# Pinning the second half of an encoder block to its source order and writing it as one pipeline of block pairs

## The chip, the cores and the metric

The kernel runs on one core of one Trainium2 chip. The metric is the device time of one execution in microseconds (us). Before the change it is 1429.65 us, the median of 3 runs (1428.54 to 1430.14).

## The reference

One layer of an encoder works on x, 256 tokens by 2048 channels, all in float32. Cut to what matters:

```
h    = rms_norm(x, g_mix)
proj = h @ w_in                        # q, k, v of three token mixers, and three gates of 2048
oa, ob, oc = mixer A (dilated windows), mixer B (grouped heads, rotary), mixer C (256 memory tokens)
gates  = sigmoid(gt)                   # (256, 3, 2048)
merged = gates[0]*(oa @ w_br_a) + gates[1]*(ob @ w_br_b) + gates[2]*(oc @ w_br_c)
x  = x + merged @ w_o
hf = rms_norm(x, g_ffn) @ w_ffn_in     # 2 x 5632 columns
x  = x + (silu(hf[:, :5632]) * hf[:, 5632:]) @ w_ffn_out
```

## The kernel before, in words

Every matrix product is cut into column blocks of 512 and runs over k tiles of 128 rows. To keep float32 accuracy each operand is split in two halves that TensorE takes at full rate: `split` (lines 83 to 91) lets ScalarE copy the source into the upper half (`hi`) and then lets VectorE subtract it from the source to get the lower half (`lo`). One product of a k tile is three matmuls: upper by upper, upper by lower, lower by upper. Weights come raw from memory on SyncE's queue (SP) and are split on the way; `whi` and `wlo` have four buffers of two k tiles each.

`product` (lines 161 to 188) computes one column block for the 256 tokens, which are two row tiles (t = 0, 1), in two banks of PSUM. It loads 1 MB (four k tiles) at a time into one of three `raw` buffers. Line 157 is the load, lines 86 and 87 the split, lines 183 to 185 the matmuls. After every k tile it calls `tick`, which lets a background job (attention, say) trace its next few instructions.

The stages in order: the memory tokens' keys and values (`w_mem`); eight blocks of q, k, v with attention in the background (`w_qkv`); twelve blocks of gates, each followed by a short branch product (`w_gate`, `w_br`), a sigmoid and a merge into `mg`; four blocks of the output projection (`w_o`), each followed by an add to x, squares for the norm, and transposes into x1T; eleven feed-forward blocks in three groups (4, 4, 3), each group followed by four blocks of `w_ffn_out`. The loop over gates has three passes, one for each branch: A (k tiles 0 and 1 of the attention output oT), C (2 to 5), B (6 to 11). The second pass begins at 380.9 us, the output projection at 612.2, the feed-forward part at 711.2.

A feed-forward block (`in_seven`, lines 525 to 615) makes 512 columns of both halves of hf at once, from 16 k tiles in eight units of two. For three of the units (`SEVEN`) the 2 by 2 arrangement of two row tiles and two column blocks is computed with seven products in place of eight. Those need stationary sums of x1T (`stationary_forms`, lines 507 to 523) and, on VectorE, sums of weights: t3, a sum into `raw`, t2 and t4. The other five units are plain ("d"). The strings `ORDER` and `ORDER0` give the order of the units; "6", "7" and "4" are the products that take t2, t3 and t4. At the end six adds and subtractions (lines 609 to 614) bring the partial sums X, Y, Z, W, V, Q together, then come SiLU (line 623), the product of the two halves (line 624), transposes (line 229) and a split into hT. PSUM is given out anew before this part: seven banks for sums, one for transposes.

The order in which each engine issues its instructions isn't that of the source: a planner that simulates the time (`schedule_with_timeline_sim=True`) takes, on each engine, what it expects to be ready. Once planned, the order on an engine is fixed, and an instruction that waits holds up all behind it.

Of the kernel before, what the change touches and what calls it, by code (L numbers as in the profile page):

```python
# [18 lines left out]
P = 128  # L19
# [8 lines left out]
PK, LOAD = 2, 4  # L28
# [24 lines left out]
ORDER = "s0 d3 s1 d4 s2 d5 6 d6 7 d7 4".split()  # L53
ORDER0 = "d3 d4 d5 s0 s1 d6 s2 6 d7 7 4".split()
# [3 lines left out]
def encoder_block(ctx: ExitStack, tc: tile.TileContext, a: dict, out: bass.AP):  # L58
    nc = tc.nc
# [6 lines left out]
    banks = ExitStack()  # L66
    pools = {"mm": banks.enter_context(tc.tile_pool(name="pmm", bufs=4, space=bass.MemoryType.PSUM)),
             "at": banks.enter_context(tc.tile_pool(name="pat", bufs=4, space=bass.MemoryType.PSUM))}
# [7 lines left out]
    def at_bank(name):  # L76
        return pools["at"].tile([P, NC], F32, name=name, tag="at")

    def mm_bank(name="mm"):
        return pools["mm"].tile([P, NC], F32, name=name, tag="mm")  # L80
# [69 lines left out]
    def load(src, k0, nk):  # L150

        raw = wp.tile([P, LOAD, NC], F32, name="raw")
        if nk % PK:
            c = k0 % PK * NC
            nc.sync.dma_start(out=raw[:, 0], in_=src[k0 // PK][:, c:c + NC])
        else:
            nc.sync.dma_start(out=raw[:, :nk].rearrange("p (u k) n -> p u (k n)", k=PK),
                              in_=src[k0 // PK:(k0 + nk) // PK].rearrange("u p n -> p u n"))
        return raw

    def product(src, lhs, nk, head=(), beside={}):


        ps = [mm_bank() for _ in range(T)]
        k0 = 0
        while k0 < nk:
            n = head[0] if head else min(LOAD, nk - k0)
            head = head[1:]
            if k0 in beside:
                start(beside[k0])  # L170
            lhs(k0)
            raw = load(src, k0, n)
            for b in range(0, n, PK):
                m = min(PK, n - b)
                hi = wp.tile([P, PK, NC], F32R, name="whi", bufs=4)
                lo = wp.tile([P, PK, NC], F32R, name="wlo", bufs=4)
                split(hi[:, :m], lo[:, :m], raw[:, b:b + m])
                for i in range(m):
                    k = k0 + b + i
                    xh, xl = lhs(k)  # L180
                    for t in range(T):
                        c = slice(t * P, (t + 1) * P)
                        nc.tensor.matmul(ps[t], lhsT=xh[:, c], rhs=hi[:, i], start=(k == 0), stop=False)  # L183
                        nc.tensor.matmul(ps[t], lhsT=xh[:, c], rhs=lo[:, i], start=False, stop=False)  # L184
                        nc.tensor.matmul(ps[t], lhsT=xl[:, c], rhs=hi[:, i], start=False, stop=(k == nk - 1))  # L185
                    tick()
            k0 += n
        return ps
# [34 lines left out]
    def transposed(src, dst, g=None):  # L223

        for h in range(2):
            tp = at_bank("tp")
# [16 lines left out]
    make_identity(nc, ident)  # L243
# [23 lines left out]
    def biases():  # L267
# [7 lines left out]
        for g in range(3):  # L275
# [4 lines left out]
            ps = at_bank("bias_ps")  # L280
# [19 lines left out]
    def take_slots(ps, slots, r, name="x", eng=nc.gpsimd):  # L300
# [38 lines left out]
        if n:  # L339
# [14 lines left out]
            for j in range(n):  # L354
                tp = at_bank("hT")
# [10 lines left out]
    def attend(qs, ks, vs, bias, kt):  # L366
# [5 lines left out]
        for i in range(g):  # L372
            sc = at_bank("sc")
# [29 lines left out]
        def turn(i):  # L403
            tp = at_bank("pT")
# [9 lines left out]
        ops = at_bank("o")  # L414
# [27 lines left out]
    first = product(a["w_mem"][0], memT, KT, (1, 1) + (2,) * 7, {6: row_sums(a["mem"], r_m, 3, "mem")})  # L442
# [3 lines left out]
    start(take_slots(product(a["w_mem"][1], memT, KT, (2,) * 8), MEM_SLOTS[4:], r_m, "mem"))  # L446
# [9 lines left out]
    mg = [s8([P, D], f"mg{t}", F32) for t in range(T)]  # L456
    for b, (g0, k0, k1) in enumerate(((0, 0, 2), (8, 2, 6), (4, 6, 12))):
        if b == 2:
            finish()
            heads.close()  # L460
            tail = ctx.enter_context(tc.tile_pool(name="tail", bufs=4))
            mT = [s8([P, 2, 4, S], "mT", pool=tail) for _ in range(4)]
        for j in range(4):
            n0 = j * NC
            gp = product(a["w_gate"][g0 + j], xT, KT)
            sg = s4([P, T, NC], "sg")
            for t in range(T):
                nc.scalar.activation(sg[:, t], gp[t], AF.Sigmoid, scale=r_x[:, 0, t:t + 1])
            bp = product(a["w_br"][j][k0 // PK:k1 // PK], lambda k: ol(k0 + k), k1 - k0)
            for t in range(T):  # L470
                m = mg[t][:, n0:n0 + NC]
                if b == 0:
                    nc.vector.tensor_mul(m, bp[t], sg[:, t])
                else:
                    nc.vector.tensor_mul(sg[:, t], bp[t], sg[:, t])
                    nc.vector.tensor_add(m, m, sg[:, t])
            if b == 2:
                transposed([mg[t][:, n0:n0 + NC] for t in range(T)],
                           lambda k, n: (mT[j][:, 0, k:k + n], mT[j][:, 1, k:k + n]))


    x = [s8([P, D], f"x{t}", F32) for t in range(T)]
    for t in range(T):
        nc.sync.dma_start(out=x[t], in_=a["x"][t * P:(t + 1) * P, :])
    x1T = [s8([P, 2, 4, S], "x1T") for _ in range(4)]
    ss1 = const.tile([P, T, 4], F32, name="ss1")
    for n in range(4):
        op = product(a["w_o"][n], lambda k: (mT[k // 4][:, 0, k % 4], mT[k // 4][:, 1, k % 4]), KT)
        junk = s4([P, T, NC], "junk")
        for t in range(T):  # L490
            xc = x[t][:, n * NC:(n + 1) * NC]
            nc.vector.tensor_add(xc, op[t], xc)
            nc.scalar.activation(junk[:, t], xc, AF.Square, accum_out=ss1[:, t, n:n + 1])
        transposed([x[t][:, n * NC:(n + 1) * NC] for t in range(T)],
                   lambda k, m: (x1T[n][:, 0, k], x1T[n][:, 1, k]),
                   lambda k: gT[:, 2, 4 * n + k:4 * n + k + 1])
    ssr = small.tile([P, T], F32, name="ss", bufs=1)
    nc.vector.tensor_reduce(ssr, ss1, axis=AX.X, op=ALU.add)
    row_scale(ssr, r_f)
# [3 lines left out]
    banks.close()  # L503
    pools["mm"] = ctx.enter_context(tc.tile_pool(name="pm2", bufs=7, space=bass.MemoryType.PSUM))
    pools["at"] = ctx.enter_context(tc.tile_pool(name="pa2", bufs=1, space=bass.MemoryType.PSUM))

    def stationary_forms():
# [15 lines left out]
        return lambda u, f: (fh[:, f, u], fl[:, f, u])  # L523

    def in_seven(src, lhs, forms, order):

        dest = {"s": "XYZW", "6": "X", "7": "X", "4": "V"}
        left = {}
        for o in order:
            for b in ([dest["s"][0], "Y", "Z", "W"] if o[0] == "s" else ["Y", "V", "Z", "Q"] * 2 if o[0] == "d"
                      else [dest[o]] * SEVEN):
                left[b] = left.get(b, 0) + 1
        ps = {}
        SA = s4([P, 2, NC], "SA")
        SB = s4([P, 2, NC], "SB")

        def mul(b, st, hi, lo):
            first = b not in ps
            if first:
# [175 lines left out]
```

## Time and profile before

| what | value |
|---|---|
| median of 3 runs | 1429.65 us |
| the profiled execution | 1432.02 us, its span 1430.2 us |
| mean granted clock of TensorE | 0.994 |
| memory traffic | 273.05 MB read, 2.88 MB written, 193 GB/s over the span |
| VectorE, lower halves of weights from raw (line 87) | 497 splits, 612.6 us |
| ScalarE, upper halves of weights from raw (line 86) | 497 splits, 524.0 us |

PE is TensorE's matmul row, PEld its loading of stationary tiles, DVE VectorE, ACT ScalarE, POOL GpSimd, SP SyncE. A row of a timeline gives the start, the duration, the engine, the line, the operation and what it writes and reads; in brackets stands how long the engine sat idle before it and what ended that. A matmul's duration spans more than its share of PE, since the next one starts before it ends: the distance from start to start is what it costs. A row of a waits view gives the total, the number of times and the longest. A row of the view by stretches gives the stretch, its length, busy us and instructions of PE, PEld, DVE, ACT and POOL, the granted clock, the share of DMA and GB/s.

### The profile page before, as it was taken

To read this page: it belongs to the slowest core of one execution; us is meant where nothing else is said; L and a number is where in the kernel's file an instruction comes from. 1 tells how busy PE (TensorE), PEld (TensorE's weight loads), DVE (VectorE), ACT (ScalarE), POOL (GpSimd) and SP (SyncE) were. 2 spreads that over 40 slices of the span, in tenths; PEclk is the share of its full clock that TensorE was granted. 3 is DMA by queue.
4 is the path that set the end of the run, shared out by engine and by line. 5 is a ranking of instruction groups with operands and counts; after the bars stand their busy time and mean duration, and the time that the engine had idled before them with its cause. 6 is when DMAs were issued, how large, how long until landed. Compare 5 with 4: busy or idle time off the path is not lost.

```text
span 1430.2 us, 16503 instructions
## 1 busy us (share of the span) xinstructions
PE 1400.4 (98%) x6323; PEld 1151.6 (81%) x6323; DVE 963.3 (67%) x1191; ACT 741.0 (52%) x971; POOL 78.8 (6%) x146
## 2 busy tenths in 40 slices
PE   6999999999999999999899999999999999999998
PEld 4778788888888888888687788888888888888887
DVE  5666776754455555555688987557988855788763
ACT  5576556544444444444456555435655643456542
POOL 0012642200000000000000000000000000000000
PEclk8999999999999999999999999999999999999999
DMA  8876445456555555655455554555554555655562
GB/s 293 272 255 187 147 175 176 135 218 217 195 180 202 191 169 188 213 181 179 174 177 180 211 186 188 187 195 206 201 186 176 203 206 190 222 176 178 206 223 101
DMA packets 64510, 276.99 MB, mean 194 GB/s; under 512 B 5232, under 2 KB 7792, under 8 KB 52912
## 3 DMA queue, kind: packets, MB, share of 16 engines
q1 hardware_dynamic: 61984, 271.73, 54.8%
q10 hardware_dynamic: 2448, 4.22, 0.9%
q8 instruction: 49, 0.80, 0.2%
q14 instruction: 29, 0.24, 0.0%
HBM read 273.05 MB, written 2.88 MB: 193 GB/s over the span
## 4 chain that ended last, share of the span: by engine, by line
PE 89%; DMA 4%; POOL 2%; DVE 2%; ACT 2%; issue 1%; SPq 0%; ACTq 0%; DVEq 0%; POOLq 0%
PE mm L184 18%; PE mm L183 18%; PE mm L185 18%; PE mmY L549 2%; PE mmY L550 2%; PE mmY L548 2%; PE mmZ L549 2%; PE mmZ L550 2%; PE mmZ L548 2%; PE mmV L549 2%; PE mmV L550 2%; PE mmV L548 2%; PE mmQ L550 2%; PE mmQ L549 2%; PE mmQ L548 2%; PE mmX L549 1%
## 5 line engine op out<-in xcount | busy, mean ns | idle before, releaser
L87 DVE TENSOR_TENSOR wlo<-raw,whi 128x1024 fp32r<-128x1024 f32 (+1 forms) x497 | 612.6, 1238 | 393.4 <-ACT whi L86 392.1
L86 ACT ACTIVATE whi<-raw 128x1024 fp32r<-128x1024 f32 (+1 forms) x497 | 524.0, 1061 | 573.5 <-PE mm L185 367.1
L183 PE MATMUL mm<-whi,xT 128*128 128x512 f32 x640 | 250.6, 393 | 1.4 <-ACT whi L86 1.1
L184 PE MATMUL mm<-wlo,xT 128*128 128x512 f32 x640 | 250.2, 391 | 1.1 <-DVE wlo L87 1.1
L185 PE MATMUL mm<-whi,xT 128*128 128x512 f32 x640 | 249.5, 391 | 0.0
L183 PEld LDWEIGHTS mm<-whi,xT 128*128 128x128 f32 x640 | 120.1, 188 | 26.7 <-ACT whi L86 1.6
L184 PEld LDWEIGHTS mm<-wlo,xT 128*128 128x128 f32 x640 | 120.2, 188 | 26.3 <-DVE wlo L87 1.5
L185 PEld LDWEIGHTS mm<-whi,xT 128*128 128x128 f32 x640 | 120.2, 188 | 24.6
L184 PE MATMUL mm<-wlo,hT 128*128 128x512 f32 x352 | 138.0, 393 | 0.0
L185 PE MATMUL mm<-whi,hT 128*128 128x512 f32 x352 | 137.6, 393 | 0.0
L183 PE MATMUL mm<-whi,hT 128*128 128x512 f32 x352 | 134.9, 391 | 0.0
L184 PEld LDWEIGHTS mm<-wlo,hT 128*128 128x128 f32 x352 | 66.1, 188 | 14.8
L183 PEld LDWEIGHTS mm<-whi,hT 128*128 128x128 f32 x352 | 66.1, 188 | 14.6
L185 PEld LDWEIGHTS mm<-whi,hT 128*128 128x128 f32 x352 | 66.1, 188 | 13.6
L87 DVE TENSOR_TENSOR wlo<-t,whi 128x1024 fp32r<-128x1024 f32 x66 | 62.9, 955 | 6.3 <-ACT whi L86 3.6
L548 PE MATMUL mmY<-whi,x1T 128*128 128x512 f32 x143 | 57.7, 403 | 5.6 <-DVE rs_h L96 5.6
L86 ACT ACTIVATE whi<-t 128x1024 fp32r<-128x1024 f32 x66 | 55.6, 843 | 10.9 <-PE mmX L550 5.7
L549 PE MATMUL mmY<-wlo,x1T 128*128 128x512 f32 x143 | 56.7, 397 | 0.1
L550 PE MATMUL mmY<-whi,x1T 128*128 128x512 f32 x143 | 56.3, 393 | 0.0
L548 PE MATMUL mmV<-whi,x1T 128*128 128x512 f32 x143 | 56.2, 393 | 0.0
L549 PE MATMUL mmV<-wlo,x1T 128*128 128x512 f32 x143 | 55.9, 391 | 0.0
L550 PE MATMUL mmV<-whi,x1T 128*128 128x512 f32 x143 | 55.9, 391 | 0.0
(192 smaller groups left out, 2117.5 us busy)
## 6 DMA issues: line engine op xcount, KB each, us to landing
raw<-in_w_ffn SPq DMA_DIRECT2D x88, 1024.0 KB, 4.9
raw<-in_w_gate SPq DMA_DIRECT2D x48, 1024.0 KB, 5.0
raw<-in_w_ffn_out SPq DMA_DIRECT2D x44, 1024.0 KB, 5.0
raw<-in_w_qkv SPq DMA_DIRECT2D x32, 1024.0 KB, 5.0
raw<-in_w_o SPq DMA_DIRECT2D x16, 1024.0 KB, 4.9
raw<-in_w_br SPq DMA_DIRECT2D x8, 1024.0 KB, 5.0
raw<-in_w_mem SPq DMA_DIRECT2D x15, 512.0 KB, 4.7
raw<-in_w_br SPq DMA_DIRECT2D x8, 512.0 KB, 3.5
```

Of the source, the lines that this page charges most:

```text
L86: nc.scalar.activation(hi, src, AF.Copy)
L87: nc.vector.tensor_sub(lo, src, hi.bitcast(F32))
L183: nc.tensor.matmul(ps[t], lhsT=xh[:, c], rhs=hi[:, i], start=(k == 0), stop=False)
L184: nc.tensor.matmul(ps[t], lhsT=xh[:, c], rhs=lo[:, i], start=False, stop=False)
L185: nc.tensor.matmul(ps[t], lhsT=xl[:, c], rhs=hi[:, i], start=False, stop=(k == nk - 1))
L548: nc.tensor.matmul(ps[b], lhsT=st[0], rhs=hi, start=first, stop=False, skip_group_check=chain)
L549: nc.tensor.matmul(ps[b], lhsT=st[0], rhs=lo, start=False, stop=False, skip_group_check=chain)
L550: nc.tensor.matmul(ps[b], lhsT=st[1], rhs=hi, start=False, stop=stop, skip_group_check=chain)
```

## The change

From the second gate pass on every instruction is pinned: it may not be issued before any that stands ahead of it in the source on the same engine. This part is rewritten so that the source order is the order wanted. It is a stream of steps. Each step has a part that makes its halves ready (load, sums, split) and a part with its matmuls; the matmuls of a step are traced after the next three steps have been made ready (`AHEAD`). Plain products run as pairs of column blocks: a step is two k tiles of one block, the blocks take turns. A unit of seven is three steps: `first` (products X, Y), `second` (three adds, then W, Z) and `third` (one add, then V); the table t4 is gone, its sum is made in place. `done` is called behind the matmuls of a pair's last steps, and the work behind it (`later`) is handed out by ticks, one step each.

Also: loads are 512 KB into six buffers, everywhere; PSUM is four banks "mm" and four "at" throughout, and X, Y, W take "at" banks; the stationary forms are built when the second column block of the output projection is transposed; the load of x moves from the planner's choice to the head of the output projection; the row factor r_f of the second half is no longer applied to the product of the halves but in the output add; the feed-forward weights lie in memory as alternating 512 KB blocks of the two halves.

```
-PK, LOAD = 2, 4
+PK = 2
-ORDER = "s0 d3 s1 d4 s2 d5 6 d6 7 d7 4".split()
-ORDER0 = "d3 d4 d5 s0 s1 d6 s2 6 d7 7 4".split()
+ORDER = "d3 s0 d4 s1 d5 s2 6 d6 7 d7".split()
+ORDER0 = "d3 s0 s1 s2 6 7 d4 d5 d6 d7".split()
+AHEAD = 3
...
+            def issue(*args, **kw):
+                ins = op(*args, **kw)
+                if self.owner.on:
+                    self.owner.tc.keep_in_program_order(ins)
+                return ins
...
-    pools = {"mm": banks.enter_context(tc.tile_pool(name="pmm", bufs=4, space=bass.MemoryType.PSUM)),
-             "at": banks.enter_context(tc.tile_pool(name="pat", bufs=4, space=bass.MemoryType.PSUM))}
+    psum = ctx.enter_context(tc.tile_pool(name="psum", bufs=4, space=bass.MemoryType.PSUM))
...
-        raw = wp.tile([P, LOAD, NC], F32, name="raw")
+        raw = wp.tile([P, PK, NC], F32, name="raw", bufs=6)
+        c = k0 % PK * NC
+        nc.sync.dma_start(out=raw[:, :nk].rearrange("p k n -> p (k n)"), in_=src[k0 // PK][:, c:c + nk * NC])
...
+        def finish_seven():
+            SA, SB = tl["A"], tl["B"]
+            nc.vector.tensor_sub(SB[:, 0], ps["Z"], SB[:, 0])
+            nc.vector.tensor_add(SA[:, 1], ps["V"], SA[:, 1])
+            nc.vector.tensor_add(SA[:, 0], ps["Y"], SA[:, 0])
+            nc.vector.tensor_add(SB[:, 1], ps["Q"], SB[:, 1])
+            return SA, SB
+
+        def whole(u, c):
+            def ready():
+                hi, lo = halves(load((src(u, c),), 0, PK))
+
+                def products():
+                    for k in range(2):
+                        for t in range(T):
+                            mul(("YV", "ZQ")[c][t], at(2 * u + k, t), hi[:, k], lo[:, k])
+                return products
+            return ready
...
+        def first(u):
+            def ready():
+                b1, b2 = (load((src(u, c),), 0, PK) for c in range(2))
+                held[u] = b1, b2
+                hi, lo = halves(b1)
...
+        def second(u):
+            def ready():
+                b1, b2 = held[u]
+                nc.vector.tensor_add(t3[:, u], b2[:, 0], b2[:, 1])
+                nc.vector.tensor_add(b2[:, 0], b2[:, 0], b1[:, 0])
+                nc.vector.tensor_add(t2[:, u], b2[:, 0], b2[:, 1])
+                hi, lo = halves(b2)
...
+        def third(u):
+            def ready():
+                b1 = held.pop(u)[0]
+                nc.vector.tensor_add(b1[:, 1], t2[:, u], b1[:, 1])
+                hi, lo = halves(b1[:, 1])
+                return lambda: mul("V", at(2 * u + 1, 1), hi[:, 0], lo[:, 0])
+            return ready
...
+        nc.on = True
+        waiting = []
+        for p in pairs:
+            for products in p:
+                waiting.append(products)
+                if len(waiting) > AHEAD:
+                    waiting.pop(0)()
+                    tick()
...
+                    elif n + c == 1:
+                        yield 2
+                        stationary_forms()
...
+                def hidden(av, bv):
+                    tl = s8([P, 2, 4, S], "hT", pool=tail)
+                    hT.append(tl)
+                    for t in range(T):
+                        nc.scalar.activation(av[:, t], av[:, t], AF.Silu, scale=r_f[:, 0, t:t + 1])
+
+                    def later():
+                        yield 2
+                        nc.vector.tensor_mul(av, av, bv)
+                        yield 2
+                        yield from transposed([av[:, t] for t in range(T)],
+                                              lambda k, m: (tl[:, 0, k:k + m], tl[:, 1, k:k + m]), lag=2)
+                    start(later())
...
+                            nc.vector.scalar_tensor_tensor(x[t][:, o], r[t][:, h * w:(h + 1) * w],
+                                                           r_f[:, 0, t:t + 1], x[t][:, o],
+                                                           op0=ALU.mult, op1=ALU.add)
...
-        "w_ffn": np.concatenate([_blocks(f[:, :DFF]), _blocks(f[:, DFF:])], -1),
+        "w_ffn": _pairs(_blocks(f[:, :DFF]), _blocks(f[:, DFF:])),
```

416 lines of the change are left out of this document (230 added, 186 removed).

## The prediction

> **What bounds the kernel now.** I read the page first, then who waited for whom on TensorE (PE), then busy time by stretch, then the timelines of PE, VectorE (DVE) and ScalarE (ACT) in one feed-forward block.
>
> ```profile
> span 1430.2 us, 16503 instructions
> PE 1400.4 (98%) x6323; PEld 1151.6 (81%) x6323; DVE 963.3 (67%) x1191; ACT 741.0 (52%) x971; POOL 78.8 (6%) x146
> PE   6999999999999999999899999999999999999998
> PE 89%; DMA 4%; POOL 2%; DVE 2%; ACT 2%; issue 1%; SPq 0%; ACTq 0%; DVEq 0%; POOLq 0%
> ```
>
> PE is the bound: 98% busy, 89% of the chain that ended last. The change alters the number of neither matmuls nor transposes, so it can only move PE's waits. They are few:
>
> ```profile
> PE mm L183 <- ACT memT L89: 13.4, 3, 7.0
> PE mmY L548 <- DVE rs_h L96: 5.6, 1, 5.6
> ...
> PE mmX L548 <- ACT whi L86: 0.9, 1, 0.9
> PE mmW L549 <- DVE wlo L87: 0.5, 1, 0.5
> ```
>
> The 13.4 us lie at the start, which is not pinned. The 5.6 us are the one gap between output projection and feed-forward. By stretch (busy us and instructions of PE, PEld, DVE, ACT, POOL; granted clock; DMA):
>
> ```profile
> 0.00:20.00 20.00, 7.12 (x24) 5.36 (x24) 6.27 (x17) 12.01 (x21) 0.70 (x6) 0.89 0.84 316
> 380.90:1425.90 1045.00, 1037.21 (x4614) 852.50 (x4612) 719.90 (x798) 524.71 (x589) 0.00 (x0) 1.00 0.54 189
> 704.00:720.00 16.00, 10.13 (x38) 8.04 (x39) 15.34 (x37) 7.31 (x12) 0.00 (x0) 0.79 0.25 86
> 755.00:770.00 15.00, 14.09 (x64) 11.09 (x63) 15.00 (x19) 9.36 (x10) 0.00 (x0) 1.00 0.63 220
> 770.00:888.00 118.00, 117.22 (x524) 95.87 (x523) 99.59 (x116) 70.29 (x83) 0.00 (x0) 1.00 0.53 187
> 1026.20:1068.90 42.70, 42.70 (x193) 34.98 (x192) 37.81 (x44) 25.74 (x30) 0.00 (x0) 1.00 0.56 196
> ```
>
> The last row is one seven-product block: PE never waits, and DVE is 37.8 of 42.7 us busy. That second number decides this case: DVE has 4.9 us of slack per block, and its order in a block is what the change fixes.
>
> **Prices.** PE: the two matmuls below are 18 apart, so one takes 4.08/18 = 0.227 us; a transpose takes 0.11.
>
> ```profile
> 559.81 0.39 PE L184 MATMUL mm<-wlo,xT 128*128 128x512 f32 x1
> ...
> 563.89 0.39 PE L184 MATMUL mm<-wlo,xT 128*128 128x512 f32 x1
> ```
> ```profile
> 852.88 0.27 PE L229 MATMUL tp<-ident,SB 128*128 128x128 f32 x1
> 852.99 0.27 PE L229 MATMUL tp<-ident,SA 128*128 128x128 f32 x1
> ```
>
> A step of the new pipeline so costs PE 2.72 us (whole: 12 matmuls), 1.36 (first, second: 6), 0.68 (third: 3), 1.36 and 0.68 (rest).
>
> ```profile
> 840.54 0.69 DVE L583 TENSOR_TENSOR t<-raw 128x512 f32<-128x512 f32 x1
> 841.15 0.68 DVE L613 TENSOR_TENSOR SB<-mmZ,SB 128x512 f32<-128x512 f32 x1
> ...
> 843.61 1.22 DVE L87 TENSOR_TENSOR wlo<-raw,whi 128x1024 fp32r<-128x1024 f32 x1
> 844.75 0.68 DVE L612 TENSOR_TENSOR SB<-mmV,SB 128x512 f32<-128x512 f32 x1
> ```
>
> Back to back, DVE spends 0.60 us on 512 columns and 1.14 on 1024; the result is there 0.69 and 1.22 after the start.
>
> ```profile
> 836.10 0.62 ACT L86 ACTIVATE whi<-t 128x512 fp32r<-128x512 f32 x1
> ```
> ```profile
> 823.09 1.06 ACT L86 ACTIVATE whi<-raw 128x1024 fp32r<-128x1024 f32 x1 [1.42 <-PE mmV L550]
> ```
> ```profile
> 824.19 1.23 DVE L87 TENSOR_TENSOR wlo<-raw,whi 128x1024 fp32r<-128x1024 f32 x1 [1.54 <-ACT whi L86]
> ```
> ```profile
> 854.91 0.68 DVE L584 TENSOR_TENSOR raw<-raw 128x512 f32<-128x512 f32 x1
> ```
> ```profile
> 855.71 1.06 ACT L86 ACTIVATE whi<-raw 128x1024 fp32r<-128x1024 f32 x1 [0.92 <-DVE raw L584]
> ```
>
> ACT needs 1.06 or 0.62 us for the upper half. A hand-over from ACT to DVE takes 824.19 - 824.15 = 0.04 us, from DVE to ACT 855.71 - 855.59 = 0.12; I take 0.04 and keep 0.12 as the upper end.
>
> **What the change gives.** The stationary forms are now built during the second half of the output projection, and the first block starts with x1T tiles that are long ready. What lay late in 704 to 720 goes: 30 matmuls and 8 transposes are worth 7.7 us there, so 8.3 of 16.0 us were lost, the 5.6 us wait and a slow clock (0.79) after it. The Trainium skill (TensorE: Matmul & The Clock Gate, "Why this matters for your kernels") says that PE idle for more than some 3 us falls to half clock; the trace agrees (0.79 after a 5.6 us gap). With 755 to 770 (0.9) and 770 to 888 (0.8) the pinned part can give back 10.0 us. Next late is then DVE.
>
> **What one unit of seven costs DVE in the pinned order.** "second" is three adds, then the split; "third" is an add, then the split. Nothing of DVE's may slip in while ACT makes the upper half:
> - first: 1.14.
> - second: adds 1.80. ACT starts when the second add ends, for 1.06; DVE has only the third add meanwhile and waits 0.5; lower half 1.14. Together 3.44.
> - third: add 0.60; 0.09 until its result is there, 0.04, 0.62 on ACT, 0.04: it waits 0.8; lower half 0.60. Together 2.00.
> - The upper half of the step behind it is queued on ACT behind that of "third": 0.4 more.
>
> That is 7.0 us of DVE for 15 matmuls (3.40 us of PE). In the block before, other steps' splits stood in those waits.
>
> **One block, from the end of the block before it.** DVE then waits at its four adds for PE's last step, and behind them is queued all that follows; PE has the three steps ready: 2.72 + 2.72 + 1.36 = 6.8 us. DVE, summed up to the split of the step d6 behind the "6" products: four adds 2.4; second 3.44; product of the two halves 1.14; third 2.00; d4 0.4 + 2.28; two splits of transposes 1.20; first, second, third 6.58; d5 0.4 + 2.28; again 6.58; "6" 0.4 + 1.74; d6 0.4 + 1.14: 32.4 us. PE wants that split after 6.8 + second, third 2.04 + transposes 0.88 + d4 5.44 + 3.40 + d5 5.44 + 3.40 + "6" 2.04 = 29.4 us. PE is 3.0 us short. From there whole steps (DVE 1.14, PE 2.72) let DVE catch up, but only to three steps ahead, so each block pays again. Eight blocks follow another: **+24.0 us**. Blocks 4 and 8 follow output products; there neither 2.4 + 1.14 + 1.20 nor the transposes lie in the way, and they pay nothing.
>
> **First block.** Its order has three units in a row. DVE up to the first split of d4: adds of the projection 1.2; 3.44 + 2.00; twice 0.4 + 6.58; "6" and "7" 0.4 + 3.48 + 0.6; 1.14; and the last column blocks' work.
>
> ```profile
> 707.91 0.86 DVE L90 SCALAR_TENSOR_TENSOR x1T<-tp,gT,x1T 128x256 fp32r<-128x256 f32 x2
> ...
> 712.07 0.16 DVE L104 SCALAR_TENSOR_TENSOR rs_y<-rs_t,rs_y 128x2 f32<-128x2 f32 x1
> 712.27 0.16 DVE L102 SCALAR_TENSOR_TENSOR rs_t<-rs_y 128x2 f32<-128x2 f32 x1
> ```
>
> Eight splits of 0.43 make 3.4, 15 small steps of the row scale at 0.20 make 3.0. Sum 32.6 us; PE has 6.8 + 2.04 + 6.80 + 4.08 + 0.9 = 20.6. **+12.0 us**. Single waits there may reach 3 us. By the rule of that page of the Trainium skill the clock would then fall again, an estimated 2 us more (what 704 to 720 lost beyond its waits); the sum leaves it out.
>
> **Smaller parts.** Hand-over at the second gate: DVE's first pinned split stands behind the two products that wait for the last branch matmul: two at 0.60, then 1.22, against 0.2 us of PE's work: **+2.5**. Banks: a block's Z and Q need two freed ones 2.72 us after the old block's end; the adds free them after 0.7 and 1.3; cover gone, some 1 us per block. Stationary forms: 3.6 + 1.5 + 1.8 us of DVE time in whole steps with 8.2 us ready: nothing; else up to 3. The fourth table, the scale folded into the output adds and the tail: below 0.5 either way.
>
> ```profile
> 304.23 0.93 SPq L484 DMA_DIRECT2D x<-in_x  x2
> ```
>
> The x loads move on SP's queue from here to the projection: 2 MB while DMA is 0.54 busy, behind six loads already issued: nothing; cover gone, up to 5.
>
> The unpinned start gets six load buffers of half the size. It holds 12.9 us of idle PE in its first 20, put down to memT behind ACT's row sums. Deeper prefetch may take some 5 us off; row loads behind more weight loads may cost as much. I take **-1**.
>
> ```profile
> raw<-in_w_ffn SPq DMA_DIRECT2D x88, 1024.0 KB, 4.9
> ...
> raw<-in_w_mem SPq DMA_DIRECT2D x15, 512.0 KB, 4.7
> ```
>
> Half the size lands hardly sooner. A buffer is then held 4.7 + 1.06 + 1.22 = 7.0 us, six of them pass a load each 1.2 us, and a block wants one each 42.4/16 = 2.65. So loads stay hidden.
>
> **Sum.** -10.0 + 24.0 + 12.0 + 2.5 - 1 = +27.5 us. The profiled execution took 1432.0 us (span 1430.2 and 1.8 around it), 2.4 above the median; on the median, 1429.65 + 27.5 = **1457 us**. With 0.12 us for each of the four hand-overs of a unit a block pays 3 x 4 x 0.08 = 1.0 more, with none 0.5 less: 1452 to 1467; with the start's 5 us, its own range is 1448 to 1471.
>
> **Rivals.** (a) *DVE keeps ahead, and it gets faster.* Place: the stretch of 32.4 against 29.4 us. If the three units' waits cost DVE 2 us a block and not 5.1, PE is never short. For it: the same DVE work fitted before with 4.9 us over, and PE did not wait. Against: those waits were filled before. Then the 10.0 us are gained and some of the 2.5 paid: 1420. (b) *Only the first block is short.* If other blocks pay under 0.5: -10 + 12 + 2.5 + 4 - 1 = +7.5, 1437. For it: every split has three steps of cover on paper. (c) *Loads become the bound.* It decides when a load takes 13.6 us to land (six buffers, 2.65 us each, less 2.3 of use). At 15 us it would be 3.7 us a block: 1457 + 11 x 3.7 = 1498. The Trainium skill (DMA: Bandwidth & Descriptors, "Bandwidth") asks for transfers of 1 MiB or more for 75% of the peak, which speaks against halved loads; the 4.7 us above do not bear it out at this depth. (d) *The pins change little*, since the orders agree or the planner finds the same waits: 1430, give or take 4.
>
> **Chances.** Forecast 0.58, (a) 0.20, (b) 0.13, (c) 0.04, (d) 0.05. The 10 us at stake below are 0.7%; a measurement of this kernel tells about 0.2% (2.9 us) from no change. (d) divides into 0.02 faster, 0.02 same, 0.01 slower; the edge of (b) and of the forecast adds 0.03 to same. Faster 0.22, same 0.05, slower 0.73. The range reaches down to the middle of (a), so that half of it is left out, as are (c) and what lies above 1472: 1420 to 1472.
>
> **What would show it.** Right: no wait on DVE rs_h between projection and feed-forward; the three steps' products in strict turns; consecutive blocks of 45 to 46 us, and DVE less than 84% busy in them while PE waits for wlo in "third", d4, d5, d6; a first block of some 54 us; output stages without waits. Wrong: blocks of 42.7 us with PE solid (then the waits on DVE were hidden, rival a), PE waiting for the adds of a finished block or for DMA, or a lower clock without a gap before it.

## The result and the profile after

The kernel after the change takes **1491.8 us**, the median of 4 runs (1491.02 to 1494.04); the kernel before took 1429.89 us beside it (4 runs, 1428.54 to 1433.88). The ratio is 1.043, interval 1.0407 to 1.0454: **slower by 62 us**, where the prediction said slower by 27.5 and at most 1472. The direction was right and so was the mechanism inside the blocks. Two places that the prediction had put at about nothing, a price that was too low, and a fall of the clock that its sum left out make up the rest.

The head of the page of the profile after:

```profile
span 1492.3 us, 17246 instructions
PE 1425.7 (96%) x6323; PEld 1152.6 (77%) x6323; DVE 973.9 (65%) x1191; ACT 734.3 (49%) x982; POOL 79.8 (5%) x146
PE   5999999999999999999799999999999999999998
PE 77%; DVE 9%; ACT 6%; DMA 4%; issue 2%; POOL 2%; ACTq 0%; SPq 0%; DVEq 0%; POOLq 0%
```

PE has as many instructions as before, but its share of the chain falls from 89 to 77%, and what comes up is DVE (2 to 9) and ACT (2 to 6). That is the picture of an engine that waits briefly, and often, for prepared operands. All instructions of the pinned kernel carry line 70, the helper that keeps their order, so one reads by tiles. What PE waited for (total us, times, longest):

```profile
PE mm L70 <- ACT memT L70: 18.3, 4, 9.3
PE tp L70 <- DVE hT L70: 10.8, 8, 1.4
PE mmY L70 <- DVE wlo L70: 5.0, 9, 1.8
PE mmX L70 <- DVE wlo L70: 3.3, 11, 0.5
PE mm L70 <- ACT y L70: 3.1, 1, 3.1
PE mmW L70 <- ACT whi L70: 3.0, 1, 3.0
PE mmW L70 <- DVE x1T L70: 2.8, 1, 2.8
PE tp L70 <- DVE SA L70: 2.6, 8, 0.3
PE mmQ L70 <- DVE x L70: 2.4, 1, 2.4
PE tp L70 <- DVE x1T L70: 1.5, 1, 1.5
```

The wait for rs_h is gone, as predicted. Note the counts: 8 times for the transposes (tp), once in each of the eight blocks that follow another block; 9 and 11 for mmY and mmX behind wlo, about once in each of the eleven.

To see where the 62 us arose, cut both executions at the first matmul of each stage. The columns are the stretch and its length, then busy us of PE, PEld, DVE, ACT and POOL, granted clock, DMA share, GB/s. Before:

```profile
0.00:62.62 62.62, 48.74 (x193) 38.30 (x193) 37.92 (x82) 37.99 (x65) 0.70 (x6) 0.92 0.82 286
380.92:612.20 231.28, 231.28 (x1033) 191.60 (x1032) 124.41 (x122) 102.44 (x106) 0.00 (x0) 1.00 0.56 191
612.20:711.18 98.98, 92.94 (x426) 76.00 (x424) 58.56 (x72) 47.26 (x67) 0.00 (x0) 0.99 0.54 187
711.18:885.22 174.04, 172.35 (x756) 140.80 (x757) 148.59 (x184) 102.46 (x118) 0.00 (x0) 0.99 0.52 182
974.03:1143.59 169.56, 169.50 (x758) 139.40 (x756) 144.41 (x167) 100.67 (x117) 0.00 (x0) 1.00 0.55 195
1232.39:1359.04 126.65, 126.65 (x566) 104.37 (x565) 106.60 (x123) 74.92 (x87) 0.00 (x0) 1.00 0.55 195
1359.04:1430.20 71.16, 66.99 (x297) 54.63 (x295) 35.19 (x37) 24.48 (x25) 0.00 (x0) 0.99 0.47 163
```

After, the same stages:

```profile
0.00:75.47 75.47, 53.51 (x192) 40.99 (x193) 39.03 (x84) 38.55 (x67) 0.71 (x6) 0.89 0.75 260
393.66:626.13 232.47, 230.71 (x1026) 190.68 (x1024) 125.30 (x121) 101.14 (x104) 0.00 (x0) 1.00 0.64 203
626.13:718.35 92.22, 91.81 (x417) 75.19 (x416) 55.85 (x62) 43.38 (x57) 0.00 (x0) 1.00 0.58 183
718.35:918.27 199.92, 181.11 (x774) 141.21 (x772) 157.62 (x196) 104.69 (x133) 0.00 (x0) 0.97 0.52 167
1007.08:1189.47 182.39, 174.50 (x758) 137.91 (x756) 150.18 (x172) 98.28 (x120) 0.00 (x0) 1.00 0.58 182
1278.28:1414.49 136.21, 130.83 (x566) 103.28 (x565) 111.77 (x128) 73.15 (x89) 0.00 (x0) 1.00 0.57 181
1414.49:1492.30 77.81, 69.45 (x297) 55.66 (x295) 36.02 (x38) 24.34 (x25) 0.00 (x0) 0.98 0.41 143
```

The rows are: the memory tokens (up to the first matmul on xT), the rest of gates and branches behind the second gate, the output projection, the three feed-forward groups of 4, 4 and 3 blocks, and the last four blocks of the output product with the tail. Set against the prediction's terms (us):

| place | forecast | measured | from the rows |
|---|---|---|---|
| start, up to the second gate | -1 | +12.7 | 393.66 - 380.92 |
| hand-over at the second gate | +2.5 | +1.2 | 232.47 - 231.28 |
| projection and the gap behind it | -8.3 | -6.8 | 92.22 - 98.98 |
| group 1 (first block 12.0, three others 9.0, less 1.7) | +19.3 | +25.9 | 199.92 - 174.04 |
| groups 2 and 3 (five blocks that follow a block) | +15.0 | +22.4 | (182.39 - 169.56) + (136.21 - 126.65) |
| last output product and tail | 0 | +6.6 | 77.81 - 71.16 |
| sum | +27.5 | +62.0 | spans: 62.1 |

So 13.7 of the missing 34.6 us lie at the start, 6.6 at the end and 14.0 in the blocks. The stretches that the table leaves out are level: the first two output products take 88.81 us each, as before.

**A block.** One whole block of group 2:

```profile
1057.46:1103.89 46.43, 43.96 (x191) 34.61 (x192) 38.39 (x45) 25.14 (x31) 0.00 (x0) 1.00 0.58 183
```

46.43 us against 42.70 before (42.39 on average in group 2 of before, 169.56/4), and DVE 38.39/46.43 = 83% busy: both are what the prediction gave as signs ("45 to 46 us", "less than 84%"). DVE's timeline in it (start, us, instruction; in brackets the idle time ahead of it and what ended that):

```profile
1073.81 0.69 DVE L70 TENSOR_TENSOR t<-raw 128x512 f32<-128x512 f32 x1
1074.54 0.69 DVE L70 TENSOR_TENSOR raw<-raw 128x512 f32<-128x512 f32 x1
1075.26 0.69 DVE L70 TENSOR_TENSOR t<-raw 128x512 f32<-128x512 f32 x1
1076.49 1.23 DVE L70 TENSOR_TENSOR wlo<-raw,whi 128x1024 fp32r<-128x1024 f32 x1 [0.54 <-ACT whi L70]
1077.63 0.68 DVE L70 TENSOR_TENSOR raw<-t,raw 128x512 f32<-128x512 f32 x1
1079.10 0.69 DVE L70 TENSOR_TENSOR wlo<-raw,whi 128x512 fp32r<-128x512 f32 x1 [0.78 <-ACT whi L70]
1080.04 1.83 DVE L70 TENSOR_TENSOR wlo<-t,whi 128x1024 fp32r<-128x1024 f32 x2 [0.26 <-ACT whi L70]
```

This is "second", "third" and the step behind them. The three waits are 0.54, 0.78 and 0.26 us where the prediction had 0.5, 0.8 and 0.4. What it had too cheap are the adds: the first starts 0.73 us before the second (1073.81, 1074.54), not 0.60. These adds hang on each other: the second overwrites what the first reads, and the third reads what the second wrote. That this is the reason fits the rows, but no run tried it by itself. "second" so lasts 3.82 us (1073.81 to 1077.63; forecast 3.44), "third" 2.15 (to 1080.04 less the wait of 0.26; forecast 2.00).

**The start.** ACT's timeline in the memory stage of after:

```profile
28.64 1.06 ACT L70 ACTIVATE whi<-raw 128x1024 fp32r<-128x1024 f32 x1 [2.58 <-PE mm L70]
29.60 0.90 ACT L70 ACTIVATE memT<-rawT,gT 128x256 fp32r<-128x256 f32 x2
35.35 1.06 ACT L70 ACTIVATE whi<-raw 128x1024 fp32r<-128x1024 f32 x1 [4.85 <-PE mm L70]
36.31 0.89 ACT L70 ACTIVATE memT<-rawT,gT 128x256 fp32r<-128x256 f32 x2
```

A split of weights waits for PE to give back one of the four whi buffers, and the memT tile that PE itself waits for stands behind it. The trace of before has no such wait in this stage.

But PE loses only 1.55 and 1.54 us behind these two memT tiles. Of the 12.9 us that the first matmul on xT comes later, PE is idle for 8.1 (75.47 - 53.51 against 62.62 - 48.74) and busy for 4.8 more with the same work, at a lower clock (0.89 for 0.92). Of the idle time, 2.3 us belong to the longest wait for memT (9.3 us, before 7.0), which is over at 23.35 us, ahead of both rows, and 2.9 to the wait for y at the end (3.1 us, before 0.2), which ACT makes behind an xT tile for whose load it waits 4.3 us.

**The end.** SP's queue in the last output product of after, and ACT's first split behind the hole:

```profile
1446.08 1.00 SPq L70 DMA_DIRECT2D out<-x  x2
1447.18 0.41 SPq L70 DMA_DIRECT2D raw<-in_w_ffn_out  x1
1454.37 0.99 SPq L70 DMA_DIRECT2D out<-x  x2
1455.45 10.82 SPq L70 DMA_DIRECT2D raw<-in_w_ffn_out  x9
```
```profile
1460.77 1.06 ACT L70 ACTIVATE whi<-raw 128x1024 fp32r<-128x1024 f32 x1 [8.35 <-DMA raw<-in_w_ffn_out]
```

The write of an output block waits on SP for the add that makes it. Pinned, it stands ahead of the loads that were traced after it; from 1447.59 to 1454.37 SP issues nothing, and nine loads go out in one row afterwards. PE waits for 4.0 us in this stage, and the clock falls to 0.83 in the 10 us from 1450 on.

### The profile page after: what moved, and what is told of

Read it like the earlier page. It is cut to its first block, busy times and chain, and to the rows that moved or that the text cites. A ratio compares the mean times of both kernels' runs of the same rounds, so it can differ in the third digit from the quotient of the medians.

```text
span 1492.3 us, 17246 instructions
## 1 busy us (share of the span) xinstructions
PE 1425.7 (96%) x6323; PEld 1152.6 (77%) x6323; DVE 973.9 (65%) x1191; ACT 734.3 (49%) x982; POOL 79.8 (5%) x146
## 4 chain that ended last, share of the span: by engine, by line
PE 77%; DVE 9%; ACT 6%; DMA 4%; issue 2%; POOL 2%; ACTq 0%; SPq 0%; DVEq 0%; POOLq 0%
PE mm L70 17%; PE mmY L70 14%; PE mmZ L70 13%; PE mmV L70 13%; PE mmQ L70 12%; DVE wlo L70 5%; ACT whi L70 4%; PE mmX L70 3%; DMA rawT<-in_xT 2%; DVE SA L70 1%; PE tp L70 1%; DMA raw<-in_w_mem 1%; POOL rot L70 1%; PE mmW L70 1%; DVE raw L70 1%
## 5 line engine op out<-in xcount | busy, mean ns | idle before, releaser
L70 PE MATMUL mm<-whi,xT 128*128 128x512 f32 x768 | 246.7, 396 | 3.1 <-ACT y L70 3.1
L70 PEld LDWEIGHTS mm<-whi,xT 128*128 128x128 f32 x768 | 144.4, 189 | 34.0 <-ACT y L70 3.6
L70 PE MATMUL mm<-wlo,xT 128*128 128x512 f32 x384 | 150.4, 392 | 0.0
L70 PE MATMUL mmZ<-whi,x1T 128*128 128x512 f32 x220 | 85.7, 390 | 0.0
L70 PE MATMUL mmQ<-whi,x1T 128*128 128x512 f32 x220 | 85.6, 389 | 0.0
L70 PE MATMUL mmQ<-whi,hT 128*128 128x512 f32 x176 | 70.0, 398 | 2.4 <-DVE x L70 2.4
L70 PE MATMUL mmZ<-whi,hT 128*128 128x512 f32 x176 | 70.2, 399 | 0.8 <-ACT whi L70 0.8
L70 PE MATMUL mmY<-whi,hT 128*128 128x512 f32 x176 | 69.3, 394 | 0.0
L70 PE MATMUL mmV<-whi,hT 128*128 128x512 f32 x176 | 69.1, 393 | 0.0
L70 PE MATMUL mm<-whi,memT 128*128 128x512 f32 x128 | 46.4, 445 | 18.7 <-ACT memT L70 18.3
L70 PEld LDWEIGHTS mmV<-whi,x1T 128*128 128x128 f32 x286 | 54.0, 189 | 12.6 <-ACT whi L70 1.7
L70 PEld LDWEIGHTS mmY<-whi,x1T 128*128 128x128 f32 x286 | 54.0, 189 | 10.4
```

What stands on the lines that cost most here:

```text
L70: ins = op(*args, **kw)
```

## The experiments

Each is one kernel and one execution with a profile, unless an interval is given. The kernel before took 1432.96 us beside e1 to e4, 1430.22 beside e5 to e8, 1430.11 beside e9 to e11 and 1430.55 beside e12.

**e1: the start's loads as before.** The unpinned part takes 1 MB loads into three buffers again; the pinned part keeps its 512 KB loads, into halves of those buffers.

```
-        raw = wp.tile([P, PK, NC], F32, name="raw", bufs=6)
+        raw = wp.tile([P, LOAD, NC], F32, name="raw")
...
-                hi, lo = halves(load((src(u, c),), 0, PK))
+                hi, lo = halves(load_half(src(u, c)))
```

> The changed kernel, with the loads of the kernel before in the unpinned part (1 MB into three buffers of 8 KB per partition, 512 KB while the memory tokens are done); the pinned part loads the same 512 KB pieces into the halves of the same three buffers. Theory: the six small buffers let weight loads pass the row loads on SP, and this alone costs the start 12.7 us (first matmul with xT at 75.5 us, before it 62.6). Then xT starts at 62 to 64 us, the second gate at 380 to 383 us, and the time falls by 11 to 14 us to 1478 to 1481. Rival: another arrangement of PSUM or another choice of the planner costs the start; then xT stays at 73 to 77 us and the time at 1488 to 1494.

Measured 1479.82 us. The first matmul on xT comes at 62.11 us:

```profile
62.11 0.50 PE L70 MATMUL mm<-whi,xT 128*128 128x512 f32 x1 [0.21 <-ACT y L70]
```

After has it at 75.47, before at 62.62: the loss at the start is the loads' alone, and it comes off the total.

**e5: the kernel before with the new loads only.** Nothing is pinned or rewritten; six buffers of 512 KB, w_ffn laid out to suit.

```
-        raw = wp.tile([P, LOAD, NC], F32, name="raw")
+        raw = wp.tile([P, PK, NC], F32, name="raw", bufs=6)
...
-    first = product(a["w_mem"][0], memT, KT, (1, 1) + (2,) * 7, {6: row_sums(a["mem"], r_m, 3, "mem")})
+    first = product(a["w_mem"][0], memT, KT, (1, 1), {6: row_sums(a["mem"], r_m, 3, "mem")})
```

> The kernel before with one part of the change alone: loads of 512 KB into six buffers, everywhere; no pins, the old blocks. Theory (at the start weight loads pass the row loads on SP, and nothing else is lost by halved loads): xT starts at 72 to 77 us and not at 62.6, the rest takes as long as before, 1438 to 1446 in all. Rival (halved loads cost bandwidth wherever they are used): later stages lengthen too, feed-forward blocks by over 0.5 us, 1450 or more. If the start is not slow here, it is the planner's choice in the changed kernel and not the loads: 1428 to 1434.

Measured 1448.03 us, 18 more than before:

```profile
72.98 0.50 PE L177 MATMUL mm<-whi,xT 128*128 128x512 f32 x1 [2.65 <-ACT y L318]
```

10.4 us are lost up to this matmul, and the three groups of blocks are longer by 1.5, 2.4 and 1.8 us (175.51, 171.96 and 128.47). The time lies between what theory and rival gave: the start is slow as the theory said, but the blocks are longer too, by 0.4 to 0.6 us each. The loads alone make a kernel slower that has no pins.

**e9: the row loads earlier.** At that point my theory was that the loads of the mem rows, which stand behind more weight loads on SP, hold up the row sums and so memT.

```
-    first = product(a["w_mem"][0], memT, KT, (1, 1), {6: row_sums(a["mem"], r_m, 3, "mem")})
+    first = product(a["w_mem"][0], memT, KT, (1, 1), {4: row_sums(a["mem"], r_m, 1, "mem")})
```

> After, but the four row loads of the mem rows are traced from k = 4 on, one step apart (after: from k = 6 on, three apart); six buffers and 512 KB loads stay. ScalarE's order at the start is then nearly that of before. My theory, that the start is lost because the row loads stand behind more weight loads on SP and the row sums behind them hold up memT on ScalarE: the first xT matmul comes at 62 to 66 us (after 75.5, before 62.6), and the run at 1480 to 1484 us. Rival, six buffers keep the DMA engines so full that the memT tiles land late whatever the order: 72 to 76 us, 1489 to 1493.

Measured 1487.92 us, first matmul on xT at 72.08. **That theory fell**: 3.4 of 12.9 us came back. Who waited for whom in the first 75 us shows what stayed:

```profile
ACT whi L70 <- PE mm L70: 8.7, 3, 3.3
```

ScalarE's splits still wait for PE three times. All full loads of w_mem have 512 KB in both kernels; what differs is that six may be under way and not three. That is the new theory.

**e12: four buffers.**

```
-        raw = wp.tile([P, PK, NC], F32, name="raw", bufs=6)
+        raw = wp.tile([P, PK, NC], F32, name="raw", bufs=4)
```

> After with four load buffers of 512 KB in place of six, nothing else. The 15 full loads of w_mem have 512 KB in before and after alike, so at the start only their number ahead differs (before three, after six). My theory after the run with earlier rows: six loads ahead let ScalarE split weights until its four split buffers are full, and each further split then waits for PE while memT stands behind it (2.6 and 4.9 us at 28 and 35 us of after). With four ahead at most one such wait is left: the first xT matmul at 64 to 69 us (after 75.5, before 62.6). Rival, what PE loses there lies in the order that the planner finds for the unpinned part and not in the number of loads ahead: 72 to 76 us. In the pinned part four buffers still suffice (a load every 2.65 us, held some 7 us): blocks as in after, 46.4 us, so 1480 to 1487 us by my theory and 1489 to 1493 by the rival.

Measured 1486.96 us:

```profile
65.33 0.39 PE L70 MATMUL mm<-whi,xT 128*128 128x512 f32 x1
```

Three ahead 62 us, four 65, six 75: it is the number of loads ahead. How it works was not as I expected: three waits of whi for PE are left, not one, 5.5 us in all against 7.4. The second gate comes 11.9 us earlier than in after (381.79), but the span is only 7.1 us shorter (1485.2), since the later stages pay with four buffers: groups of 200.68, 183.94 and 137.16 us, 3.3 more, and 1.5 more in the last product. That they would suffice there was wrong.

**e2: the output writes later.** The writes of the last but one pair of column blocks are traced 8 steps later, behind the loads of the last pair.

```
-                            if last:
+                            if last and n:
                                 nc.sync.dma_start(out=out[t * P:(t + 1) * P, o], in_=x[t][:, o])
+                    if last and not n:
+                        def write(c=c):
+                            yield 8
...
+                        start(write())
```

> The changed kernel, with the output writes of the last but one pair of blocks traced eight steps later. Theory: on SP these writes wait for VectorE's adds, and the weight loads of the last pair stand behind them; that costs 6.4 us in the last output stage (73.3 us; in the two output stages without such writes nothing is lost). Then the stage takes 66.5 to 67.5 us and the time falls by 5 to 7 us to 1485 to 1487. Rival: the stage is slow because its pairs are short (12 k tiles), or by banks that wait for adds; then the stage stays at 72 to 74 us and the time within 1.5 us of 1491.8.

Measured 1487.45 us. The last product with its tail:

```profile
1414.36:1485.70 71.34, 67.00 (x297) 54.68 (x295) 36.01 (x38) 24.35 (x25) 0.00 (x0) 1.00 0.47 155
```

71.34 us, against 77.81 after and 71.16 before: the whole loss of this stage is the place of four writes (two pairs) in SP's queue. The total is half a microsecond above what the theory gave.

**e3: the adds early.** All sums of a unit are made beside the split of "first", and none stands directly ahead of the split that needs it.

```
                 held[u] = b1, b2
+                nc.vector.tensor_add(t3[:, u], b2[:, 0], b2[:, 1])
+                nc.vector.tensor_add(b2[:, 0], b2[:, 0], b1[:, 0])
+                nc.vector.tensor_add(t2[:, u], b2[:, 0], b2[:, 1])
                 hi, lo = halves(b1)
+                nc.vector.tensor_add(b1[:, 1], t2[:, u], b1[:, 1])
```

> The changed kernel, with the weight sums of a unit of seven moved up: the three adds ahead of the split of 'first', the fourth right behind it. The amount of VectorE work is the same. Theory: VectorE's waits for ScalarE between an add and its split (0.45 to 0.54, 0.78 and 0.26 us a unit in the trace of the changed kernel) make it late; filled, blocks that follow a block fall from 46.6 us to 44 to 45, the first from 60 to 55 to 57, and the time by 15 to 24 us to 1468 to 1477. What is left then is VectorE's pile at a block's start. Rival: the wait of the transposes for a free bank (1.35 us a block) and the pile at the block's end make up the loss; then blocks stay at 46 to 47 us and the time falls by less than 6 us.

Measured 1467.86 us. A block of group 2:

```profile
1017.66:1062.04 44.38, 42.83 (x192) 34.98 (x192) 38.23 (x45) 25.76 (x31) 0.00 (x0) 1.00 0.54 190
```

44.38 us and not 46.43, with the same adds and splits: taking the adds out of the waits between the two engines is worth 24 us of the total. The three groups give 10.2, 7.8 and 6.0 of them.

**e7: the first block's order.** Its three units are put apart.

```
-ORDER0 = "d3 s0 s1 s2 6 7 d4 d5 d6 d7".split()
+ORDER0 = "d3 s0 d4 d5 s1 d6 s2 6 7 d7".split()
```

> The changed kernel with another order of the first block: d3 s0 d4 d5 s1 d6 s2 6 7 d7 in place of d3 s0 s1 s2 6 7 d4 d5 d6 d7. Same work. Theory (three units of seven in a row want 7 us of VectorE for each 3.4 us of PE): with whole steps between them the first block falls from 60 us to 49 to 53, the time by 7 to 11 us to 1481 to 1485. Rival (the first block is slow since the last columns of x1T and the row scale come late, whatever the order): it stays above 57 us, for d4 and d6 then wait for x1T, and the time falls by less than 3 us.

Measured 1481.9 us. Group 1 is 191.10 us (199.92), groups 2 and 3 are as after (182.41, 135.95): 8.8 us were the row of three units in the first block. They are not all waits, as the first block of after and then of this run shows:

```profile
718.35:778.71 60.36, 48.93 (x201) 37.31 (x199) 42.43 (x64) 29.25 (x40) 0.00 (x0) 0.92 0.44 139
```
```profile
715.65:767.45 51.80, 45.41 (x200) 35.43 (x199) 42.05 (x64) 28.57 (x40) 0.00 (x0) 1.00 0.49 151
```

The block is 8.6 us shorter, and 3.5 of them are busy time of PE, at a clock of 1.00 in place of 0.92. In after, matmuls with no wait between them stand 0.43 us apart from 741.66 to 751.39, elsewhere 0.23.

**e6: the second half of the transposes later.** The rival was that PE waits at the transposes for a bank (tp behind hT) and not because DVE is late.

```
-                                              lambda k, m: (tl[:, 0, k:k + m], tl[:, 1, k:k + m]), lag=2)
+                                              lambda k, m: (tl[:, 0, k:k + m], tl[:, 1, k:k + m]), lag=4)
```

> The changed kernel, with the second half of a feed-forward block's transposes traced four steps behind the first and not two, so that a bank of the 'at' group is free again. The profile of the changed kernel puts 1.35 us a block down to that wait. Theory (VectorE late in its fixed order; the wait for the bank only shows it early): PE then waits for VectorE's splits a few steps later, blocks stay at 46.0 to 46.7 us, the time within 3 us of 1491.8. Rival (the bank is a cause of its own): blocks at 45.0 to 45.4 us, the time 9 to 13 us shorter.

Measured 1493.56 us, blocks of 46.4 to 46.7 as in after. The waits of the transposes for hT are gone, and those of mmY for wlo have grown from 5.0 to 12.0 us. The bank is only where DVE's lateness shows first; take it away and it shows elsewhere.

**e4: no pins.** The rewritten kernel, with the planner free to order it.

```
-        nc.on = True
+        nc.on = False
```

> The changed kernel without a single pin: the planner chooses the order on every engine again. Theory (the fixed order on VectorE and SP is the loss, not the rewritten arithmetic): the planner fills VectorE's waits as it did before, blocks come to 42.5 to 44 us, the last output stage to 67, the start stays slow (xT at 73 to 77 us): 1437 to 1452. Rival (pairs, steps of three and halved loads cost the time by themselves): blocks stay above 45.5 us and the time above 1475.

Measured 1439.33 us. Groups of 173.59, 170.13 and 125.70 us: level with before. The start stays slow (first matmul on xT at 72.45). So the rewrite into pairs and steps costs nothing in the blocks, the pinned order does.

**e11: no pins, and the start's loads as before** (the edits of e4 and e1 together).

> After with nothing pinned at all, and the loads of the start as before; the rewrite into pairs stays. My theory, that pins and loads make the whole loss: level with before, 1426 to 1430 us. Rival, the halved loads into halves of a buffer or the rewrite cost something of their own: 1434 to 1440 us.

Measured 1421.62 us, 4 runs; ratio to before 0.9941, interval 0.9926 to 0.9957. That is better than my theory said, by over 4 us at the nearer end. In its profile the projection takes 91.53 us (98.98 before), and nothing waits for rs_h any more.

**e8: pinned, with the repairs together.** e1, e2 and e3, the first block's order of e7, and for the others:

```
-ORDER = "d3 s0 d4 s1 d5 s2 6 d6 7 d7".split()
+ORDER = "d3 d4 s0 d5 s1 d6 s2 6 7 d7".split()
```

> The changed kernel, pinned as it is, with all that the runs so far point to: the loads of the kernel before in the unpinned part, output writes eight steps later, weight sums early, the first block's order d3 s0 d4 d5 s1 d6 s2 6 7 d7 and that of the others d3 d4 s0 d5 s1 d6 s2 6 7 d7, which puts two more whole steps between a block's end and its first unit of seven. Theory: start -12.5, outputs -6.5, sums -24, first block -6, the new order -1.5 a block for eight blocks: 1427 to 1434, level with the kernel before, with blocks of 42.5 to 43.2 us. Rival (a pinned order cannot follow the hardware closely enough): blocks of 44 us or more, 1440 or more.

Measured 1437.22 us, 4 runs; ratio 1.0048, interval 1.0031 to 1.0065, and blocks of 43.70 us: both lie between what theory and rival gave. What PE still waits for there:

```profile
PE mmX L70 <- ACT SB L70: 10.5, 11, 1.0
```

Eleven times 0.95 us: my order has "7" directly behind "6", both use the bank X, and ScalarE must first copy it out.

**e10: one step between.** As e8, with the last whole pair of a block divided, in the first block's order too.

```
-ORDER = "d3 d4 s0 d5 s1 d6 s2 6 7 d7".split()
+ORDER = "d3 d4 s0 d5 s1 d6 s2 6 e7 7 f7".split()
...
+                      "e": lambda: [whole(u, 0)], "f": lambda: [whole(u, 1)],
```

> The pinned kernel of the last combination (loads of the start as before, output writes later, adds ahead of the first split, other order of a block), and the last whole pair of a block divided, so that a whole step stands between the sums 6 and 7. My theory, that the 11 waits of 0.95 us at the X bank come from 7 standing right behind 6: they go, blocks of 42.6 to 42.9 us, 1425 to 1428 us, which is 0.1 to 0.4 per cent less than before. Rival, the bank is waited for wherever 7 stands, or VectorE is short again there: 1434 to 1438, as without it.

Measured **1424.49 us**, 5 runs, just below what my theory gave; ratio to before 0.9959, interval 0.9946 to 0.9971. A block and the head of the page:

```profile
1015.27:1057.72 42.45, 42.45 (x193) 35.13 (x191) 38.02 (x45) 25.66 (x31) 0.00 (x0) 1.00 0.55 198
```
```profile
span 1420.9 us, 16928 instructions
PE 1396.5 (98%) x6323; PEld 1151.1 (81%) x6323; DVE 968.3 (68%) x1191; ACT 738.7 (52%) x982; POOL 78.9 (6%) x146
```

PE is solid through the block, with everything still pinned. Pinning as such costs little, if anything: e10 and the unpinned e11 are 2.9 us apart, and their intervals overlap. What cost the time were this order, these loads and these writes.

## Why the prediction was right, and where it failed

**Right: what decides.** The prediction said that DVE's order in a block decides, that the waits between ScalarE and VectorE which other work had filled would lie open, and that PE would come up short once a block. The waits stand in the trace within 0.14 us of their prices, e3 takes them away and gets 24 us back, and e4 shows that without the pins the blocks are level with before. "They pay nothing", said of blocks behind output products, nearly held too: the first block of group 2 took 43.09 us (1007.08 to 1050.17) and the three behind it 46.4. Rivals (a), (b) and (d) are out by the 46.43 us of a block; (c) is out because loads land in 4.0 us:

```profile
raw<-in_w_ffn SPq DMA_DIRECT2D x176, 512.0 KB, 4.0
raw<-in_w_mem SPq DMA_DIRECT2D x15, 512.0 KB, 7.0
```

1 MB took 4.9 before. The rule that the prediction weighed there (the Trainium skill, DMA: Bandwidth & Descriptors, "Bandwidth": 1 MiB or more) did not decide the blocks. The halved loads of e5 lengthen its groups by 1.2% (475.94 us for 470.25), but e10, which loads halves too, has blocks of 42.45 us; so the runs show no price that halved loads have everywhere.

**Failed: "The unpinned start ... I take -1"** (measured +12.7). The loss that it did name, "row loads behind more weight loads", is worth 3.4 us (e9); the sign and the mechanism were wrong. The prediction priced six loads ahead as a shorter way to the first tiles, or a longer one for the rows; e1, e5 and e12 show that six ahead cost 10 to 13 us there, and four 2.7. By which link they do it stays open. Two stand in the trace: ScalarE splits ahead until its four buffers are full and then waits for PE with PE's own operand behind it (2.58 and 4.85 us); and a load lands after 7.0 us where it took 4.7 (the w_mem row above). The first can't be the main one. These waits of ScalarE come to 7.4 us in after, 8.7 in e9 and 5.5 in e12, while the matmul on xT comes 12.9, 9.5 and 2.7 us late; with 5.4 and 5.2 us e4 and e5 are late by 9.8 and 10.4. The landing time does go with the loss (7.0 to 7.1 us in after, e4 and e5, 6.7 in e9, 4.9 in e12, 4.7 in e1 and before), but it also goes with the number of loads ahead, and no run parts the two. Behind the longer gaps the clock is low as well:

```profile
20.00:30.00 10.00, 5.25 (x12) 3.80 (x12) 5.50 (x17) 6.21 (x11) 0.00 (x0) 0.59 0.89 344
```

0.59 of full speed after PE's wait of 9.3 us. The rule of the Trainium skill cited in the prediction (TensorE: Matmul & The Clock Gate) agrees with this row.

**Failed: "the tail: below 0.5 either way" and "output stages without waits"** (measured +6.6). The prediction followed the x loads past SP's queue, but not the output writes. A write that waits on SP for its data holds every load behind it. e2 settles it. In the first two output products, which have no such writes, the sign held.

**Too small: "eight blocks x 3.0"** (measured 3.7 against the block shown, 4.0 against the mean of 42.39). The term of the unit is at fault: 7.0 us, of which "second" 3.44 and "third" 2.00. With the measured 3.82, 2.15 and 0.26 a unit is 1.14 + 3.82 + 2.15 + 0.26 = 7.4, three of them 1.2 more, and 3.0 becomes 4.2. The prediction took the 0.60 us of two adds that don't depend on each other for a chain that does. It also placed PE's waits at wlo in third, d4, d5 and d6. Some are there (8.3 us at mmY and mmX), but PE waited more at the transposes, whose operands and banks DVE frees in the same queue (10.8 us behind hT and 2.6 behind SA, 8 times each). The shortage was the same, the place only in part.

**Too small: "First block +12.0"**. Group 1 lost 25.9 where 19.3 were forecast, and its first block took 60.36 us where the prediction gave some 54. Three things that the sum lacked stand in the trace: the dearer units, 1.2 us in each of the four blocks; the two waits for x1T (2.8 and 1.5 us), which come from the stationary forms and transposes that the prediction put at nothing and "else up to 3"; and the clock, which the prediction named, put at 2 us and left out of the sum, and which cost about 3.5 (the two rows at e7). Together they are more than the missing 6.6, so how it divides among them isn't shown. The prediction tied the clock to single waits that reach 3 us; the longest ahead of the fall was 2.84, and 11 us lay between the two. e7 confirms that the order costs the larger part: 8.8 us back from the order alone, the clock's share with it.

**Nearly right:** the gap behind the projection gave 6.8 us (8.3 forecast); the hand-over at the second gate cost 1.2, with a single wait of 1.8 us in the trace (2.5 forecast).

**The range** was too narrow for one reason: the unknowns at start and end were bounded by 5 and 0.5 us, from rows that priced the transfer and not the queue behind it. With the 14.0 us of the blocks alone the time would have been 1471 and inside the range.

## What to carry to other kernels

When an order is pinned, count on the engine with the least slack the hand-overs to other engines that nothing fills any more, with dependent instructions at their dependent price; then spread them so that other work lies between a result and its use. More loads under way are no gain by themselves: here six ahead made the start 12.7 us longer than three, so the depth is worth trying both ways. In every queue that issues in order put the instructions that wait for late results (here the output writes) behind the loads of the next stage.

## What was not expected of the hardware

- Adds of 128x512 on VectorE of which one needs or overwrites what the other works on start 0.72 us apart (1074.54 to 1075.26), independent ones 0.61 (840.54 to 841.15 in the rows of before that the prediction shows).
- The clock of TensorE fell in the first block of after, from about 741 us on, although no single wait ahead of it was longer than 2.84 us; waits of 2.84, 1.48, 0.68 and 1.31 us lay in the 13 us ahead of it. In e7, with waits of 2.84 and 1.49 us at the same place and then 10 us of solid matmuls, it stayed at 1.00.
- A 512 KB load landed in 4.0 us in the feed-forward blocks where 1 MB took 4.9, so half the size gave back a fifth of the time, and with six loads under way at the start it took 7.0 where three took 4.7.
- The pinned e10 and the unpinned e11 are both faster than before, 1424.49 and 1421.62 us; what both gain for certain is the gap behind the projection (92.21 and 91.53 us for 98.98). Both also reach the second gate 3.2 us earlier than before (377.71 and 377.69 for 380.92); where these 3.2 us come from was not looked into.
